# Three of eleven down-projection weight tiles of each expert multiplied in fp32 instead of as fp16 pairs

## The chip, the cores and the metric

The kernel runs on one core of one Trainium2 chip. The metric is the device time of the whole program in microseconds; lower is better. A time is the median of several runs; the profile is of one execution, whose own time stands beside its span.

## The reference, cut to what matters

A two-layer diffusion trunk over 256 latent and 256 context tokens of width 1024. The change touches the last part alone, the second layer's mixture of experts over the 256 latent tokens: eight SwiGLU experts, two for each token, each expert with a gate/up matrix (1024 x 5632) and a down matrix (2816 x 1024) in fp32.

```python
def swiglu(h, w_gu, w_dn):
    gate, up = jnp.split(h @ w_gu, 2, axis=-1)
    return (jax.nn.silu(gate) * up) @ w_dn
...
    top_logit, top_e = lax.top_k(logits, TOP_K)
    top_w = jax.nn.softmax(top_logit, axis=-1)
...
    yb = lax.map(lambda a: swiglu(a[0], w_gu[a[1]], w_dn[a[1]]), (xb, block_expert))
    yb = yb.reshape(n_rows, D) * row_w[:, None].astype(h.dtype)
    return jax.ops.segment_sum(yb, src_tok, num_segments=n).reshape(B, L, D)
```

## The kernel before, in words

**Products.** All large products of the kernel are made of three fp16 products. An fp32 operand is split into a high half (its fp16 rounding) and a low half (the rest, in fp16), and TensorE adds high x high, high x low and low x high. `split` (L264 to L268) does this for any tile: ScalarE writes the high half (`wh`, `hdh`, `yh`; line L267 in the profile), then VectorE, from the source and the high half, writes the low half (`wl`, `hdl`, `yl`; line L264 there, that of the helper `stt`).

**Weights.** The experts' weights come as tiles of 128 x 2048 fp32, 1 MB each, 33 for an expert: 22 for gate and up (one for each 128 of the 2816 hidden columns) and 11 for down. The SyncE queue loads them in order into raw buffers (twelve in the experts' part: `raw`, `raw2`, `raw3`, and the two of `hh` and `hl`); a raw buffer is free again when the split of its tile is done. A split tile is a pair of fp16 buffers, and there are `WB` = 3 such pairs, in rotation: a tile's split can begin when the pair of the tile three before it has been used by TensorE for the last time.

**One expert** (`expert`) has two stages. Gate-up: for each of 11 pairs of tiles TensorE forms gate and up for 256 hidden columns over the expert's 96 token slots (`CAP`), 48 products a tile (L320 to L322, 128x96 each). ScalarE applies SiLU (`ht`, L1220), VectorE multiplies by up (`ht`, L258), and a split writes `hdh` and `hdl`, two chunks of 128 at a time. Down: 44 chunk steps, 22 for each half of 512 output columns, four to a tile; in each the stationary operand is a chunk of the activations (128 x 96) and the moving one 128 x 512 of the weights, three products a step (L1239 to L1241). At the end of each half a split, scaled by the routing weight, writes `yh` and `yl`.

**Around it.** `gather` picks the next expert's 96 tokens by a one-hot product (`P`, `wsl`, `xg`; VectorE, TensorE and ScalarE) and is called from the middle of the down stage. `combine` adds the outputs of several experts back to the tokens: after experts 2, 5 and 6 eight jobs, one for each 128 columns, each with products (L1256) and one VectorE row (`xT`); they are handed to the next expert, which takes one for each pair of tiles. Expert 7 combines its own two halves at once. Each engine runs its instructions in an order fixed when the kernel is built. The builder works from the program's order but may move an instruction ahead where its inputs are ready, as it does with parts of `gather` and `combine`.

The part under `If(most > CAP)` handles an expert with over 96 tokens.

Of the kernel before, what the change touches and what calls it, by code (L numbers as in the profile page):

```python
# [7 lines left out]
FT = mybir.dt.float32  # L8
F16 = mybir.dt.float16
# [11 lines left out]
NF = 22  # L21
NE = 8
CAP = 96
VW = 416
WS = 2.0 ** 10
AS = 2.0 ** 3
PSC = 2.0 ** 10
US = 1.0 / (WS * AS)
EPS = 1e-6
# [70 lines left out]
def tile_width(name):  # L100
    if name in ("v0", "v1"):
        return 4 * VW
    if name == "up":
# [107 lines left out]
def moe_tiles(w_gu, w_dn, w_router):  # L211


    g = w_gu.reshape(NE, KD, 128, 2, NF, 128)
    g = g.transpose(0, 4, 2, 3, 1, 5).reshape(NE, NF, 128, 2048)
    d = w_dn.reshape(NE, 22, 128, 2, 512).transpose(0, 3, 1, 2, 4).reshape(NE, 11, 4, 128, 512)
    d = d.transpose(0, 1, 3, 2, 4).reshape(NE, 11, 128, 2048)
    return np.concatenate([g, d], axis=1).reshape(-1), np.ascontiguousarray(_blocks(w_router)).reshape(128, 64)

# [28 lines left out]
def trunk(tc, A, out):  # L248
    nc = tc.nc
    V, S, T, G = nc.vector, nc.scalar, nc.tensor, nc.gpsimd  # L250
    cnt = [0]

    def nm(p="t"):
        cnt[0] += 1
        return f"{p}{cnt[0]}"

    def mul(o, a, b):
        V.tensor_tensor(o, a, b, op=OP.mult)  # L258
# [7 lines left out]
    def split(hi, lo, src, scale):  # L266
        h = S.activation(hi, src, AF.Copy, scale=scale)  # L267
        stt(lo, src, scale, hi, OP.mult, OP.subtract)  # L268
        return h
# [31 lines left out]
    def load_raw(name, off, w=2048):  # L301
        raw = new_raw()
        nc.sync.dma_start(raw[:, :w], dram(name, off, w))
        return raw
# [4 lines left out]
    def split_w(raw, w, parts=None, step=1024):  # L309
        if parts is None:  # L310
            pool, tag, n = take("wb", wb_slots)
            parts = [pool.tile([128, 2048], F16, tag=tag + h, bufs=n, name=nm("w" + h)) for h in "hl"]
        hi, lo = parts
        for a in range(0, w, step):
            b = min(w, a + step)
            issued[0] = split(hi[:, a:b], lo[:, a:b], raw[:, a:b], WS)
        return hi, lo
# [268 lines left out]
    def mixer(pool, i, ada_q, nrm, nxt, first=None):  # L586
# [141 lines left out]
        def value(t):  # L728
            ps = pa()[:, :VW]
            ts_ = slice(t * 128, t * 128 + 128)  # L730
# [446 lines left out]
    def gather(pool, pos_e, w_e, slots):  # L1177
# [26 lines left out]
        return wsl, xg, PT  # L1204

    def expert(pool, wsl, xg, tile_of, jobs, meanwhile, halves=(lambda *y: None,) * 2):


        hdh = pool.tile([128, NF, CAP], F16, tag="hd", bufs=2, name=nm("hdh"))
        hdl = pool.tile([128, NF, CAP], F16, tag="hd", bufs=2, name=nm("hdl"))  # L1210
        for b in range(11):
            ps = pa([128, 2, 2, CAP])
            for j in range(2):
                w = tile_of(2 * b + j)
                for a in range(2):
                    for k in range(KD):
                        c = slice(1024 * a + 128 * k, 1024 * a + 128 * k + 128)
                        prod(ps[:, j, a], w[0][:, c], w[1][:, c], xg[:, k, 0], xg[:, k, 1], k == 0, k == KD - 1)
            t_ = pool.tile([128, 2, CAP], FT, tag="ht", bufs=3, name=nm("ht"))
            S.activation(t_, ps[:, :, 0], AF.Silu, scale=US)  # L1220
            mul(t_, t_, ps[:, :, 1])
            split(hdh[:, 2 * b:2 * b + 2], hdl[:, 2 * b:2 * b + 2], t_, US * AS)
            if jobs:
                jobs.pop(0)()
        while jobs:
            jobs.pop(0)()
        yh = pool.tile([CAP, D], F16, tag="yh", bufs=4, name=nm("yh"))
        yl = pool.tile([CAP, D], F16, tag="yl", bufs=4, name=nm("yl"))
        res = None
        for j in range(44):  # L1230
            n, f = divmod(j, NF)
            if j % 4 == 0:
                w = tile_of(22 + j // 4)
            if j == 12:
                res = meanwhile()
            if f == 0:
                py = pg()[:CAP]
            c = slice(512 * (j % 4), 512 * (j % 4) + 512)
            T.matmul(py, hdh[:, f], w[0][:, c], start=(f == 0), stop=False)  # L1239
            T.matmul(py, hdh[:, f], w[1][:, c], start=False, stop=False)  # L1240
            T.matmul(py, hdl[:, f], w[0][:, c], start=False, stop=(f == NF - 1))  # L1241
            if f == NF - 1:
                split(yh[:, 512 * n:512 * n + 512], yl[:, 512 * n:512 * n + 512], py, wsl[:, 0:1])
                halves[n](yh, yl)
        return yh, yl, res
# [29 lines left out]
    with tc.tile_pool(name="mo", bufs=1, reuse_waits="tile") as pool:  # L1275
        for t, raw in enumerate(ahead):
            nc.sync.dma_start(raw, dram("wm", t * 128 * 2048, 2048))
        raw_slots.extend([(px, "raw3", 1), (pool, "raw2", 5)])
        routed = route(pool)
        with tc.issue_after(n_f1.end.ins), tc.issue_after(routed.ins):  # L1280
            first = [split_w(ahead[0], 2048)]
        raw_slots.extend([(st, "hh", 1), (st, "hl", 1)])
        ys = []

        def moe_w(e, t):
            if e == 0 and t < len(ahead):
                return split_w(ahead[t], 2048) if t else first[0]
            return split_w(load_raw("wm", (33 * e + t) * 128 * 2048), 2048, step=2048)

        def slots_of(e):  # L1290
            return gather(pool, lambda t: posm[:, t, e:e + 1], lambda t: wsel[:, t, e, :], slot)

        ys, jobs = [], []
        with tc.issue_after(issued[0].ins):
            g = slots_of(0)
        for e in range(NE):
            wsl, xg, PT = g
            if e == NE - 1:
                nrm = Norm(1, 0, [(2, 4)])
                expert(pool, wsl, xg, lambda t: moe_w(e, t), jobs, lambda: None,  # L1300
                       [lambda yh, yl, n=n: [job() for job in combine([(yh, yl, PT)], nrm)[4 * n:4 * n + 4]]
                        for n in range(2)])
                break
            yh, yl, g = expert(pool, wsl, xg, lambda t: moe_w(e, t), jobs, lambda: slots_of(e + 1))
            ys.append((yh, yl, PT))
            if e in (2, 5, NE - 2):
                jobs, ys = combine(ys), []
        finish(nrm)
        del raw_slots[1:]

    most = nc.values_load(cnti[0:1, 0:1], min_val=0, max_val=NLAT)
    with tc.If(most > CAP):
        with tc.tile_pool(name="mo2", bufs=1) as pool, tc.tile_pool(name="dr", bufs=1,
                                                                    space=bass.MemoryType.DRAM) as dp:
            dpos = dp.tile([NE, 128, 2], FT, name="dpos")
            dsel = dp.tile([NE, 128, 4], F16, name="dsel")
            for e in range(NE):
                nc.sync.dma_start(dpos[e], posm[:, :, e])
                nc.sync.dma_start(dsel[e].rearrange("p (a b) -> p a b", a=2), wsel[:, :, e, :])
            wm = A["wm"].rearrange("(e t p n) -> e t p n", e=NE, t=33, p=128)  # L1320
            for first_slot in range(CAP, NLAT, CAP):
                slot2 = pool.tile([128, 128], FT, tag="slot2", name=nm("slot2"))
                V.tensor_scalar(slot2, slot, float(first_slot), None, op0=OP.add)
                with tc.For_i(0, NE, 1) as e:
                    pe = pool.tile([128, 2], FT, tag="pe", name=nm("pe"))
                    we = pool.tile([128, 2, 2], F16, tag="we", name=nm("we"))
                    nc.sync.dma_start(pe, dpos[ds(e, 1)].rearrange("o p t -> (o p) t"))
                    nc.sync.dma_start(we.rearrange("p a b -> p (a b)"), dsel[ds(e, 1)].rearrange("o p t -> (o p) t"))

                    def tile_of(t):  # L1330
                        raw = new_raw()
                        nc.sync.dma_start(raw, wm[ds(e, 1), t].rearrange("o p n -> (o p) n"))
                        return split_w(raw, 2048)

                    wsl, xg, PT = gather(pool, lambda t: pe[:, t:t + 1], lambda t: we[:, t, :], slot2)
                    yh, yl, _ = expert(pool, wsl, xg, tile_of, [], lambda: None)
                    for job in combine([(yh, yl, PT)]):
                        job()
            nrm = Norm(1, 0, [(2, 4)])
            for k in range(KD):  # L1340
                nrm.square(0, k)
            finish(nrm)
# [22 lines left out]
```

## Time and profile before

| | us |
|---|---|
| median of 3 runs | 1804.65 (1804.35 to 1805.43) |
| the profiled execution, its own time | 1798.44 |
| span of its trace | 1796.4 |
| first product of the experts | 1085.03 |
| last product of a down stage (expert 7) | 1775.38 |
| TensorE busy in the span | 1650.2 |
| VectorE busy | 1378.0 |
| ScalarE busy | 1039.5 |

Times inside the trace are microseconds from the span's start. The profile's busy share of an engine is a mean over the whole span; what an engine is worth in a stage is read from the windows and timelines of that stage. A matmul row's end is modelled: a 128x512 fp16 product shows as 0.379 us although the next can start 0.216 after it. An fp32 product shows as two records. In a timeline the bracket at the end of a row is the time for which the engine stood idle before it, and what ended that.

### The profile page before, as it was taken

The numbers are of one execution on the slowest core, as the hardware profiler recorded it, in microseconds if no ns is written. First come the engines' busy times: TensorE is split into PE (matmuls) and PEld (weight loads), VectorE is DVE, ScalarE is ACT, GpSimd is POOL, SyncE is SP. The second block draws the span as 40 slices with busy tenths as digits, with TensorE's granted clock in tenths as the row PEclk, the third lists the DMA queues.
The fourth block names the chain that finished last, engine by engine and source line by source line (L and its number), as shares of the span: only waits on it lengthen the run. The fifth ranks groups of instructions, "written<-read, shape, count | busy, mean of one in ns | idle before, by whom it ended". The sixth has DMA issues, their size and how long they took to land.

```text
span 1796.4 us, 38098 instructions
## 1 busy us (share of the span) xinstructions
PE 1650.2 (92%) x16125; PEld 1086.6 (60%) x16125; DVE 1378.0 (77%) x2201; ACT 1039.5 (58%) x1422; POOL 1.4 (0%) x7
## 2 busy tenths in 40 slices
PE   6998899999999999999778988999999999999995
PEld 2544444446644444467556877786868686868673
DVE  4678656455886545446888678999999999999996
ACT  3456646343422322233666548888878888878783
POOL 0000000000000000000000000000000000000000
PEclk9999999999999999999989988999999999999998
DMA  9254497452465545443637668999999999999980
GB/s 384 88 150 103 105 272 196 134 190 95 148 227 188 184 162 173 167 145 101 176 77 165 191 249 327 424 414 402 418 401 388 402 417 401 422 397 401 381 373 26
DMA packets 149986, 451.95 MB, mean 252 GB/s; under 512 B 92208, under 2 KB 95408, under 8 KB 103088
## 3 DMA queue, kind: packets, MB, share of 16 engines
q1 hardware_dynamic: 149376, 449.03, 68.9%
q8 instruction: 128, 2.10, 0.5%
q14 instruction: 50, 0.41, 0.1%
q10 hardware_dynamic: 432, 0.41, 0.1%
HBM read 427.38 MB, written 1.05 MB: 238 GB/s over the span
## 4 chain that ended last, share of the span: by engine, by line
PE 45%; DVE 18%; issue 12%; DMA 12%; ACT 5%; ACTq 0%; SPq 0%; DVEq 0%
DVE wl L264 10%; DMA raw<-in_wm 7%; PE pg L320 6%; PE pg L321 6%; PE pg L322 6%; PE pa L321 6%; PE pa L322 6%; PE pa L320 5%; DMA pt<-pn 3%; ACT wh L267 3%; PE pg L1240 2%; PE pg L1241 2%; PE pg L1239 2%; PE pb L935 1%; DVE ht L258 1%
## 5 line engine op out<-in xcount | busy, mean ns | idle before, releaser
L264 DVE SCALAR_TENSOR_TENSOR wl<-raw,wh 128x2048 f16<-128x2048 f32 (+1 forms) x477 | 820.9, 1735 | 54.6 <-ACT wh L267 50.6
L267 ACT ACTIVATE wh<-raw 128x2048 f16<-128x2048 f32 (+1 forms) x477 | 686.9, 1462 | 260.1 <-PE pa L321 93.1
L322 PEld LDWEIGHTS <-wl 128*128 128x128 f16 x4346 | 428.1, 99 | 176.6 <-DVE wl L264 58.0
L320 PEld LDWEIGHTS <-wh 128*128 128x128 f16 x4346 | 429.4, 99 | 133.3 <-issue 19.0
L321 PEld LDWEIGHTS <-wh 128*128 128x128 f16 x4346 | 428.6, 99 | 117.1 <-issue 9.6
L322 PE MATMUL pa<-xg,wl 128*128 128x96 f16 x2816 | 375.7, 207 | 37.0 <-DVE wl L264 36.5
L320 PE MATMUL pa<-xg,wh 128*128 128x96 f16 x2816 | 374.7, 206 | 3.7 <-ACT wh L267 3.7
L321 PE MATMUL pa<-xg,wh 128*128 128x96 f16 x2816 | 374.6, 206 | 0.0
L320 PE MATMUL pa<-hh,wh 128*128 128x512 f16 (+1 forms) x480 | 168.0, 357 | 7.5 <-ACT hh L538 7.5
L320 PE MATMUL pg<-hh,wh 128*128 128x512 f16 (+1 forms) x512 | 171.9, 336 | 2.7 <-DVE km L264 2.1
L321 PE MATMUL pg<-hl,wh 128*128 128x512 f16 (+1 forms) x512 | 171.8, 336 | 0.0
L321 PE MATMUL pa<-hl,wh 128*128 128x512 f16 (+1 forms) x480 | 170.3, 355 | 1.5 <-DVE hl L264 1.4
L322 PE MATMUL pg<-hh,wl 128*128 128x512 f16 (+1 forms) x512 | 171.2, 334 | 0.0
L322 PE MATMUL pa<-hh,wl 128*128 128x512 f16 (+1 forms) x480 | 170.0, 355 | 0.0
L1240 PE MATMUL pg<-wl,hdh 128*96 128x512 f16 x352 | 133.4, 379 | 7.9 <-DVE wl L264 7.4
L264 DVE SCALAR_TENSOR_TENSOR scr<-raw,cb 128x1024 f16<-128x1024 f32 x64 | 78.3, 1224 | 72.2 <-DMA raw<-in_ada 71.1
L1241 PE MATMUL pg<-wh,hdl 128*96 128x512 f16 x352 | 133.3, 379 | 0.0
L1239 PE MATMUL pg<-wh,hdh 128*96 128x512 f16 x352 | 132.2, 379 | 0.0
L267 ACT ACTIVATE pn<-P,sml 128x512 f16<-128x512 f32 (+1 forms) x96 | 60.7, 645 | 30.1 <-DMA pt<-pn 19.4
L264 DVE SCALAR_TENSOR_TENSOR pn<-P,sml,pn 128x512 f16<-128x512 f32 (+1 forms) x96 | 62.0, 659 | 20.9 <-ACT pn L267 19.9
L321 PE MATMUL pg<-dl,wh 128*128 128x512 f16 (+1 forms) x198 | 70.4, 355 | 0.0
L322 PE MATMUL pg<-dh,wl 128*128 128x512 f16 (+1 forms) x198 | 70.4, 355 | 0.0
(252 smaller groups left out, 1886.7 us busy)
## 6 DMA issues: line engine op xcount, KB each, us to landing
raw<-in_wm SPq DMA_DIRECT2D x264, 1024.0 KB, 8.1
raw<-in_ws SPq DMA_DIRECT2D x52, 1024.0 KB, 4.8
raw<-in_ada SPq DMA_DIRECT2D x48, 1024.0 KB, 5.2
raw<-in_ws SPq DMA_DIRECT2D x18, 768.0 KB, 5.1
raw<-in_ws SPq DMA_DIRECT2D x16, 704.0 KB, 4.1
raw<-in_ws SPq DMA_DIRECT2D x16, 640.0 KB, 4.2
raw<-in_ws SPq DMA_DIRECT2D x4, 832.0 KB, 11.6
xT<-in_xt SPq DMA_DIRECT2D x4, 512.0 KB, 6.2
```

The source lines that it names most:

```text
L258: V.tensor_tensor(o, a, b, op=OP.mult)
L264: return V.scalar_tensor_tensor(o, a, s, b, op0=op0, op1=op1, **kw)
L267: h = S.activation(hi, src, AF.Copy, scale=scale)
L320: T.matmul(ps, sh, mh, start=first, stop=False)
L321: T.matmul(ps, sh, ml, start=False, stop=False)
L322: T.matmul(ps, sl, mh, start=False, stop=last)
L935: T.matmul(py[64 * a:64 * a + 64], (vl if m == 2 else vh)[:, kt, vc:vc + 64], pts[a][:, :, (nkt if m == 1 else 0) + kt, :], start=(kt == 0 ...
L1239: T.matmul(py, hdh[:, f], w[0][:, c], start=(f == 0), stop=False)
L1240: T.matmul(py, hdh[:, f], w[1][:, c], start=False, stop=False)
L1241: T.matmul(py, hdl[:, f], w[0][:, c], start=False, stop=(f == NF - 1))
```

## The change

Of each expert's eleven down tiles, numbers 4, 5 and 10 (`DN_RAW`) are not split: `moe_w` returns the raw fp32 buffer. The six activation chunks 16 to 21 that these tiles meet (the last three pairs of gate-up) stay fp32 as well, in a new tile `hdf`, and `hdh` and `hdl` hold 16 chunks. For these twelve of the 44 chunk steps one fp32 product takes the place of three fp16 ones. The steps of the second half of the output begin with chunks 20 and 21, so that tile 5 (chunks 20 and 21 of both halves) holds only fp32 steps; the host lays the weights out in that order (`DN_STEPS`). The scale of the sums stays what it was: `hdf` keeps both scale factors of the gate-up sums, and the raw weights carry none.

```diff
+F32_FROM = 16
+DN_STEPS = [(0, f) for f in range(22)] + [(1, f) for f in (20, 21) + tuple(range(20))]
+DN_RAW = (4, 5, 10)
...
-    d = w_dn.reshape(NE, 22, 128, 2, 512).transpose(0, 3, 1, 2, 4).reshape(NE, 11, 4, 128, 512)
+    d = w_dn.reshape(NE, 22, 128, 2, 512).transpose(0, 3, 1, 2, 4)
+    d = np.stack([d[:, n, f] for n, f in DN_STEPS], axis=1).reshape(NE, 11, 4, 128, 512)
...
-        hdh = pool.tile([128, NF, CAP], F16, tag="hd", bufs=2, name=nm("hdh"))
-        hdl = pool.tile([128, NF, CAP], F16, tag="hd", bufs=2, name=nm("hdl"))
+        hdh = pool.tile([128, F32_FROM, CAP], F16, tag="hd", bufs=2, name=nm("hdh"))
+        hdl = pool.tile([128, F32_FROM, CAP], F16, tag="hd", bufs=2, name=nm("hdl"))
+        hdf = pool.tile([128, NF - F32_FROM, CAP], FT, tag="hdf", bufs=1, name=nm("hdf"))
...
-            mul(t_, t_, ps[:, :, 1])
-            split(hdh[:, 2 * b:2 * b + 2], hdl[:, 2 * b:2 * b + 2], t_, US * AS)
+            if 2 * b < F32_FROM:
+                mul(t_, t_, ps[:, :, 1])
+                split(hdh[:, 2 * b:2 * b + 2], hdl[:, 2 * b:2 * b + 2], t_, US * AS)
+            else:
+                mul(hdf[:, 2 * b - F32_FROM:2 * b - F32_FROM + 2], t_, ps[:, :, 1])
...
-        for j in range(44):
-            n, f = divmod(j, NF)
+        for j, (n, f) in enumerate(DN_STEPS):
...
-            T.matmul(py, hdh[:, f], w[0][:, c], start=(f == 0), stop=False)
-            T.matmul(py, hdh[:, f], w[1][:, c], start=False, stop=False)
-            T.matmul(py, hdl[:, f], w[0][:, c], start=False, stop=(f == NF - 1))
-            if f == NF - 1:
+            if f >= F32_FROM:
+                T.matmul(py, hdf[:, f - F32_FROM], w[:, c], start=begin, stop=end)
+            else:
+                T.matmul(py, hdh[:, f], w[0][:, c], start=begin, stop=False)
+                T.matmul(py, hdh[:, f], w[1][:, c], start=False, stop=False)
+                T.matmul(py, hdl[:, f], w[0][:, c], start=False, stop=end)
+            if end:
...
-            return split_w(load_raw("wm", (33 * e + t) * 128 * 2048), 2048, step=2048)
+            raw = load_raw("wm", (33 * e + t) * 128 * 2048)
+            return raw if t - 22 in DN_RAW else split_w(raw, 2048, step=2048)
```

## Rows read from the trace of the kernel before

**Rows 1.** The page: busy time, share and instructions of each engine

```profile
PE 1650.2 (92%) x16125; PEld 1086.6 (60%) x16125; DVE 1378.0 (77%) x2201; ACT 1039.5 (58%) x1422; POOL 1.4 (0%) x7
```

**Rows 2.** Windows: length, PE, PEld, DVE, ACT, POOL busy, clock, DMA share, GB/s

```profile
1431.94:1485.61 53.67, 48.85 (x1073) 46.11 (x1072) 53.46 (x44) 46.10 (x45) 0.00 (x0) 1.00 1.01 419
1485.61:1516.35 30.74, 29.70 (x144) 16.95 (x142) 27.65 (x17) 23.28 (x17) 0.00 (x0) 1.00 0.99 404
...
1601.39:1657.81 56.42, 52.30 (x1117) 48.99 (x1116) 56.24 (x49) 47.34 (x48) 0.00 (x0) 1.00 0.99 392
...
1688.82:1744.05 55.23, 49.21 (x1065) 46.01 (x1064) 55.02 (x46) 45.75 (x43) 0.00 (x0) 1.00 0.99 398
```

**Rows 3.** Timeline of VectorE at the end of expert 4's gate-up: start, us

```profile
1481.04 0.35 DVE L264 SCALAR_TENSOR_TENSOR hdl<-ht,hdh 128x192 f16<-128x192 f32 x1
1481.31 2.28 DVE L264 SCALAR_TENSOR_TENSOR wl<-raw,wh 128x2048 f16<-128x2048 f32 x1
1483.51 0.35 DVE L258 TENSOR_TENSOR ht<-ht,pa 128x192 f32<-128x192 f32 x1
1483.77 0.44 DVE L1182 TENSOR_SCALAR P<-cmat,posm 128x96 f16<-128x96 f32 x2
1484.13 2.28 DVE L264 SCALAR_TENSOR_TENSOR wl<-raw,wh 128x2048 f16<-128x2048 f32 x1
```

**Rows 4.** Timeline of TensorE, the last fourteen products of that gate-up

```profile
1485.02 0.21 PE L321 MATMUL pa<-xg,wh 128*128 128x96 f16 x1
...
1485.57 0.21 PE L322 MATMUL pa<-xg,wl 128*128 128x96 f16 x1
```

**Rows 5.** Timeline of ScalarE in expert 4's down stage

```profile
1501.35 0.68 ACT L267 ACTIVATE yh<-pg,wsl 96x512 f16<-96x512 f32 x1 [2.19 <-PE pg L1241]
1501.94 5.50 ACT L267 ACTIVATE wh<-raw 128x2048 f16<-128x2048 f32 x3
...
1511.37 1.91 ACT L267 ACTIVATE wh<-raw 128x2048 f16<-128x2048 f32 x1 [0.68 <-DMA raw<-in_wm]
1513.96 1.91 ACT L267 ACTIVATE wh<-raw 128x2048 f16<-128x2048 f32 x1 [0.68 <-PE pg L1241]
```

**Rows 6.** Timelines of fp32 products and stationary loads in the first layer

```profile
21.54 1.92 PE L412 MATMUL pg<-raw,c 128*32 128x512 f32 x16
...
79.33 0.59 PE L679 MATMUL pg<-rq,cmat 128*128 128x256 f32 x2
79.76 0.34 PE L320 MATMUL pa<-wh,hh 128*128 128x416 f16 x1
...
79.15 0.37 PEld L679 LDWEIGHTS pg<-rq,cmat 128*128 128x128 f32 x2
```

**Rows 7.** Timeline of TensorE, its waits in expert 4's down stage

```profile
1486.47 0.38 PE L1240 MATMUL pg<-wl,hdh 128*96 128x512 f16 x1 [0.47 <-DVE wl L264]
...
1506.21 0.38 PE L1240 MATMUL pg<-wl,hdh 128*96 128x512 f16 x1 [0.57 <-DVE wl L264]
```

**Rows 8.** Waits between 1144 and 1776: us in total, times, longest

```profile
PE pg L1240 <- DVE wl L264: 7.4, 14, 1.0
ACT wh L267 <- DMA raw<-in_wm: 4.3, 6, 1.0
```

**Rows 9.** Timeline of VectorE at the turn to expert 4

```profile
1433.70 0.74 DVE L264 SCALAR_TENSOR_TENSOR yl<-pg,wsl,yh 96x512 f16<-96x512 f32 x1
1434.66 4.49 DVE L264 SCALAR_TENSOR_TENSOR wl<-raw,wh 128x2048 f16<-128x2048 f32 x2 [0.21 <-ACT wh L267]
1439.07 0.35 DVE L258 TENSOR_TENSOR ht<-ht,pa 128x192 f32<-128x192 f32 x1
```

**Rows 10.** Timeline of VectorE at the turns to experts 6 and 7

```profile
1606.96 0.88 DVE L264 SCALAR_TENSOR_TENSOR xT<-pb,g2s,xT 128x256 f32<-128x256 f32 x2
...
1609.96 0.35 DVE L258 TENSOR_TENSOR ht<-ht,pa 128x192 f32<-128x192 f32 x1
...
1696.73 0.35 DVE L258 TENSOR_TENSOR ht<-ht,pa 128x192 f32<-128x192 f32 x1
```

More of the change, by code (lines that the diff above doesn't have):

```diff
@@ L1235, in expert @@
                 res = meanwhile()
-            if f == 0:
+            begin, end = j % NF == 0, j % NF == NF - 1
+            if begin:
                 py = pg()[:CAP]
             c = slice(512 * (j % 4), 512 * (j % 4) + 512)
-            T.matmul(py, hdh[:, f], w[0][:, c], start=(f == 0), stop=False)
-            T.matmul(py, hdh[:, f], w[1][:, c], start=False, stop=False)
-            T.matmul(py, hdl[:, f], w[0][:, c], start=False, stop=(f == NF - 1))
-            if f == NF - 1:
+            if f >= F32_FROM:
[5 more added lines that the diff above has]
+            if end:
                 split(yh[:, 512 * n:512 * n + 512], yl[:, 512 * n:512 * n + 512], py, wsl[:, 0:1])
@@ L1332, in tile_of @@
                         nc.sync.dma_start(raw, wm[ds(e, 1), t].rearrange("o p n -> (o p) n"))
-                        return split_w(raw, 2048)
+                        return raw if t - 22 in DN_RAW else split_w(raw, 2048)
                     wsl, xg, PT = gather(pool, lambda t: pe[:, t:t + 1], lambda t: we[:, t, :], slot2)
```

## The prediction

> **What bounds the kernel now.** I read the page's busy shares first. TensorE at 92% and VectorE at 77% are means over unlike stages [rows 1], so next come the windows, cut at the first product of each expert stage. Eight experts fill the last 700 us of the span. Each is a gate-up stage (22 weight tiles) and a down stage (11 tiles), and each stage has its own limit. In expert 4's gate-up VectorE is busy 53.46 of 53.67 us, and TensorE has pauses. In its down stage TensorE is busy 29.70 of 30.74 us and VectorE 27.65 [rows 2]. The clock is at its full level (1.00, the 2.4 GHz one) in all four windows.
>
> The VectorE timeline shows what a gate-up tile costs there. From the start of a `wl` to the next row is 2.20 us, and an activation row (`ht` or `hdl`) adds 0.27. Nothing stands between them [rows 3]. TensorE's rows of the same stretch lie 0.55 us apart over thirteen steps, 42 ns a product, so a tile's 48 products take 2.04 us [rows 4]: it would be ready sooner than VectorE serves it. In the down stage a tile takes TensorE 2.59 us, the distance of two `wh` rows that each wait for it [rows 5], and that is 12 products of 0.216. VectorE's 2.20 fits inside.
>
> So a microsecond of VectorE time is worth a microsecond in gate-up and little in down, and for TensorE it is the reverse. The three tiles left unsplit are all down tiles. Between the stages time is carried only by the lead in split tiles, and `WB` = 3 pairs limit that.
>
> **Part 1: dearer products.** Per expert 12 chunk steps lose 36 fp16 products: 36 x 0.216 = 7.77 us. Each gets one fp32 product. The trace has none of 96 stationary columns, but has neighbours. A 128x256 fp32 product makes two records, and from its start to that of the next fp16 product is 79.33 to 79.76, 0.43 us [rows 6]: four passes of 256 columns at the full clock. For 512 columns that makes 0.86. The 128x512 fp32 products of the early layer take 1.92 us for 16 records [rows 6]. Four run side by side in different column groups, so less the 0.17 us of drain it is 1.75 / 4 = 0.44 per record, 0.88 a product. I take 0.86: 12 x 0.86 = 10.32, so +2.55 us per expert, **+20.4** for eight. Down is TensorE's stage, so all of it is on the path. Bounds: 0.853 (columns alone) to 0.88, or +19.7 to +22.3.
>
> Each fp32 product also loads its stationary twice. The two loads of the row take 0.37 us together [rows 6] and still fit in the 0.43 between products, so I cost them at nothing. Uncovered they would add 24 x 0.19 = 4.6 us per expert. The Trainium skill (TensorE: Matmul & The Clock Gate, Weight-path perf modes) says that the fast weight load is off for fp32, which speaks against this change. The rows agree that such a load is long, 0.19 us, and with the loads left bare the sum would be some 37 us worse; with them covered, as in the row, it stays.
>
> **Part 2: three hi/lo splits of weights removed, on ScalarE and VectorE.** 3 x 2.20 us per expert, all in the down stage, where VectorE has slack. By itself this is worth nothing there. It pays through waits:
>
> *The gap in mid-down.* ScalarE's queue holds `yh` of the first half until TensorE ends that half (2.19 us idle), and three weight splits stand behind it [rows 5]. The low half of a later tile is late by that, and TensorE stops [rows 7]. The stage has 14 such waits, 7.4 us in all [rows 8]. Four are at the first product of a down stage (0.47 us each [rows 7]) and stay, since VectorE sets both of its sides. The other ten hold 5.5 us, and each hides another 0.16, a record's 0.379 less 0.216: 7.1 us. After the change the first half ends inside raw tile 5. Tiles 4 and 5 keep TensorE busy for 8 x 0.86 = 6.9 us without a split, while the pairs of tiles 6 to 8, free since tiles 1 to 3, are filled before `yh`. Tile 9 gets tile 6's pair with tiles 7 and 8 (5.2 us) for cover, against 1.91 + 2.20. So the gap goes: **-7.1** (bounds 0 and -7.1).
>
> *The lead at the turn.* Before expert 4, gate-up begins at 1431.94. VectorE ends the second new tile only at 1433.70, does `yl`, then tiles 3 and 4, done at 1439.07, 7.13 us after the turn [rows 9]. The third must wait for the last down tile's pair. After the change the last tile is raw, so the third tile takes tile 9's pair, free 4 x 0.86 = 3.4 us before the turn, and its split is done some 1 us after it. The fourth needs the first's pair: 2.04 + 0.17 of drain, `wh` 1.91, `wl` 2.20 give 6.4 us. The gain is thus 0.7, not a whole tile. VectorE idles in between. Four turns are of this kind. In two (before experts 3 and 6) two `xT` rows of the combine stand ahead, and the fourth tile is done 8.6 us after 1601.39 [rows 10]; these rows fit into the new idle time: -2.2 each. Before expert 7 it is 1696.73 - 1688.82 = 7.9 [rows 10]: -1.5. Sum 4 x 0.7 + 2 x 2.2 + 1.5 = **-8.7** (bounds 0 and -8.7). From there on VectorE sets the pace again.
>
> **Part 3: three activation splits removed.** The `mul` stays and writes `hdf` at the same size. Of the three `hdl` one stands ahead of the last gate-up tile: 0.27 x 8 = **-2.2**. The other two fall into the down stage, where VectorE's slack hides them. Without that slack they are worth 0.5 us per expert.
>
> **Part 4: raw buffers held longer, steps reordered.** A raw tile's buffer comes free when TensorE has used it rather than at its split, three tiles later at most, and the loads of the SyncE queue behind it wait. Waits for a load come to 4.3 us over all experts [rows 8], and some are put on a load only for coming last. The stage asks less of the loads than before whenever it gets no shorter (404 to 419 GB/s now [rows 2]). Cost nothing, bound +4.3. The new order of the second half keeps the count of steps.
>
> **Sum.** 20.4 - 7.1 - 8.7 - 2.2 = +2.4 us on the profiled 1798.44, so 1800.8. The median stands 6.2 above the profiled run: 1804.65 + 2.4 = **1807.0** us, +0.13%. About 0.2% (3.6 us) is what a measurement of this kernel can tell from no change.
>
> **Rivals.**
> *A, slower: ScalarE's order keeps the lead from forming.* If `yh` of the second half is queued ahead of the third new tile's `wh`, that split waits for the turn as now. The 8.7 stay out: 1815.7. It decides once `yh` stands one place too early. For it: such an order already costs 2.19 us in mid-down [rows 5]. Against: the last tile now takes 3.4 us, in which the queue has nothing else ready. Chance 0.22.
>
> *B, faster: VectorE's new idle time in the down stage takes in small work.* Of the combine, 56.42 - 53.67 = 2.75 us of gate-up in experts 3 and 6, and 55.23 - 53.67 = 1.56 in 7 [rows 2], I have counted 1.4 and 0.8. Moved whole, the rest gives 2 x 1.35 + 0.8 = 3.5; the gather's `P` rows (0.36, seven times [rows 3]) give 2.5, the four first-product waits 4 x 0.63 = 2.5. That is -8.5: 1798.5. It decides if the instruction order puts them there, which the trace of before can't show. Chance 0.20.
>
> *C, faster: VectorE's time is the bound throughout.* Then 3 x (2.20 + 0.27) = 7.4 us per expert would come through, up to the loads: 33 x 1.049 MB at 419 GB/s are 82.6 us against 53.67 + 30.74 = 84.4. -1.8 x 8: 1790. The three pairs speak against it. Chance 0.05.
>
> *D, slower: the fp32 stationary loads are not covered*, 24 x 0.19 x 8 = +36: 1843. Chance 0.05.
>
> *E, slower: the held raw buffers starve the splits*, +4.3: 1811. Chance 0.03.
>
> **How the numbers follow.** The forecast has 0.45. Its own range is 1801 to 1812 (the bounds of product price, gap and lead partly met): 0.31 within 0.2%, 0.10 slower, 0.04 faster. A gives 0.22 slower, B 0.13 faster and 0.07 same, C 0.05 faster, D and E 0.08 slower. Together: faster 0.22, same 0.38, slower 0.40. The range takes in B and A, 1797 to 1817, and leaves out C, D and the far end of A with the gap unclosed (1822.8), some 0.15.
>
> **What would show it.** Down stages longer by some 1.6 to 1.9 us where they had a gap (near 32.6 for expert 4) and gate-ups shorter by about 1.0 (near 52.7). Two fp32 records per step of 0.43 us each, with no idle time in front. No `wl` wait in mid-down. The fourth new tile done 6.4 us after the turn, with VectorE idle for some 2 us before it. VectorE's busy time falls by 8 x 7.4 = 59 us while the span stays. The forecast is wrong if gate-up keeps its 53.7 us (A), if a down stage exceeds 34 us (D), or if the `xT` and `P` rows leave gate-up (B).

## The result and the profile after

The changed kernel takes 1815.25 us (median of five runs, 1813.31 to 1820.58) against 1804.65 for the kernel before (five runs, 1802.35 to 1807.15): a ratio of 1.0064, interval 1.0046 to 1.0081. It is slower, by 10.6 us where 2.4 were forecast. The time lies within the range that was given, and nearly on the 1815.7 of rival A; the case called likeliest did not come. That it lies within half a microsecond of A is in part chance, as the terms below show.

Before the first expert product both programs issue the same instructions in the same order, yet that product comes anywhere between 1083 and 1093 us in the fourteen profiles of this study, one of each kernel, at 1083.08 in the one of before and at 1093.39 in the one of after. So everything below is taken from the expert stage alone, first gate-up product to last down product. (The 1085.03 in the table ahead of the prediction is eighteen products late; it carried no term.) That stage took 692.68 us before and takes 704.98 after, +12.3.

The window of the whole expert stage before:

```profile
1083.08:1775.76 692.68, 643.68 (x9887) 517.03 (x9884) 659.27 (x515) 558.57 (x497) 0.00 (x0) 1.00 0.95 385
```

The windows of after: gate-up and down of expert 4, and the whole expert stage.

```profile
core 0: us, PE busy (x) PEld busy (x) DVE busy (x) ACT busy (x) POOL busy (x), PEclk, DMA share, GB/s
1448.74:1502.23 53.49, 48.67 (x1073) 46.08 (x1072) 51.42 (x42) 46.02 (x43) 0.00 (x0) 1.00 0.99 409
1502.23:1535.07 32.84, 32.23 (x133) 16.44 (x130) 22.16 (x12) 17.15 (x13) 0.00 (x0) 1.00 0.96 392
1093.39:1798.37 704.98, 662.04 (x9791) 513.05 (x9788) 599.97 (x467) 508.57 (x449) 0.00 (x0) 1.00 0.93 379
```

Against [rows 2], down went from 30.74 to 32.84, and gate-up only from 53.67 to 53.49. VectorE lost 59 us of work over the stage (659.27 before), and yet the stage got longer. Over the eight experts the gate-ups fell by 2.7 us in sum (444.9 to 442.2) where 10.9 were forecast, and the downs rose by 15.0 (247.8 to 262.8) where 13.3 were.

TensorE at the end of expert 4's down stage in after: its products, then its stationary loads.

```profile
1531.42 0.38 PE L1253 MATMUL pg<-wh,hdl 128*96 128x512 f16 x1
1531.63 3.60 PE L1249 MATMUL pg<-raw,hdf 128*96 128x512 f32 x8
1535.07 0.21 PE L324 MATMUL pa<-xg,wh 128*128 128x96 f16 x1
```

```profile
1531.20 0.12 PEld L1253 LDWEIGHTS <-hdl 128*96 128x96 f16 x1
...
1532.07 0.16 PEld L1249 LDWEIGHTS pg<-raw,hdf 128*96 128x96 f32 x1 [0.27 <-issue]
1532.49 0.16 PEld L1249 LDWEIGHTS pg<-raw,hdf 128*96 128x96 f32 x1 [0.27 <-issue]
```

Eight records from 1531.63 to 1535.07 are 0.43 each, 0.86 a product, with nothing idle in front and the next stage's first product directly behind. A load takes 0.16 of every 0.43. So the first term stands as it was made: 12 x 0.86 less 7.77, +2.55 an expert. An fp32 load of 96 columns is longer than an fp16 one (0.16 against 0.12), but lies beside the products and costs nothing here. The Trainium skill (TensorE: Matmul & The Clock Gate, Weight-path perf modes) has the fast weight load on only where the weights are 128 in number and not fp32. The trace agrees as far as it goes: the fp16 loads of 128 columns in gate-up take 0.10, less than the fp16 ones of 96. By that rule no load of this down stage is fast, fp16 or fp32, so it does not speak against this change; the prediction took it to.

ScalarE in the same down stage of after, across the turn at 1535.07.

```profile
1508.78 1.91 ACT L271 ACTIVATE wh<-raw 128x2048 f16<-128x2048 f32 x1 [1.12 <-PE pg L1253]
1519.11 0.68 ACT L271 ACTIVATE yh<-pg,wsl 96x512 f16<-96x512 f32 x1 [8.42 <-PE pg L1249]
1519.70 5.63 ACT L271 ACTIVATE wh<-raw 128x2048 f16<-128x2048 f32 x3
...
1529.24 1.91 ACT L271 ACTIVATE wh<-raw 128x2048 f16<-128x2048 f32 x1 [0.79 <-PE pg L1253]
1535.27 0.68 ACT L271 ACTIVATE yh<-pg,wsl 96x512 f16<-96x512 f32 x1 [4.11 <-PE pg L1249]
1535.85 3.70 ACT L271 ACTIVATE wh<-raw 128x2048 f16<-128x2048 f32 x2
```

This is the row that decides. Only two weight tiles of the next expert are ahead of the second `yh`; the third and fourth start at 1535.85, after it, although the third tile's pair came free when tile 9 was done, at about 1531.8. For 4.11 us ScalarE holds `yh` and waits for TensorE's last product. The first `yh` now waits 8.42 where it waited 2.19 [rows 5].

VectorE at two turns of after: to expert 1, whose first product is at 1186.04, and to expert 4 (product at 1535.07).

```profile
1190.18 4.49 DVE L268 SCALAR_TENSOR_TENSOR wl<-raw,wh 128x2048 f16<-128x2048 f32 x2 [2.48 <-ACT wh L271]
...
1535.99 0.75 DVE L268 SCALAR_TENSOR_TENSOR yl<-pg,wsl,yh 96x512 f16<-96x512 f32 x1 [2.50 <-ACT yh L271]
1537.78 4.50 DVE L268 SCALAR_TENSOR_TENSOR wl<-raw,wh 128x2048 f16<-128x2048 f32 x2 [1.05 <-ACT wh L271]
1542.20 0.35 DVE L262 TENSOR_TENSOR ht<-ht,pa 128x192 f32<-128x192 f32 x1
```

At the turn to expert 4 the row behind the fourth tile starts 7.13 us after the turn, to the hundredth what it was before the change [rows 9]. At the turn to expert 1 three `wh` happen to stand ahead of `yh`; the first of the two rows is the fourth tile's and is done 1190.18 + 2.20 - 1186.04 = 6.3 us after the turn (6.4 in the forecast, whose terms add up to 6.32), and that gate-up fell by 1.26 us (54.28 to 53.02), where those of the other experts fell by 0.14 to 0.28.

Waits in the expert stage of after: us in total, times, longest.

```profile
ACT yh L271 <- PE pg L1249: 90.3, 15, 9.1
DVE yl L268 <- ACT yh L271: 62.4, 14, 7.1
ACT wh L271 <- DMA raw<-in_wm: 3.6, 1, 3.6
PE pg L1252 <- DVE wl L268: 2.9, 7, 0.6
```

The first of them before:

```profile
ACT yh L267 <- PE pg L1241: 26.6, 15, 5.6
```

TensorE's waits for `wl` in the down stages shrank from 7.4 us in 14 [rows 8] to 2.9 in 7. In their place ScalarE stands 90 us behind `yh`, and VectorE 62 us behind ScalarE: the 59 us of removed work are now idle time.

### The profile page after: what moved, and what is told of

Its sections match the earlier page's. It is cut to its first block, busy times and chain, and to the rows that moved or that the text cites. A ratio compares the mean times of both kernels' runs of the same rounds, so it can differ in the third digit from the quotient of the medians.

```text
span 1818.5 us, 37764 instructions
## 1 busy us (share of the span) xinstructions
PE 1677.2 (92%) x16029; PEld 1087.3 (60%) x16029; DVE 1318.1 (72%) x2153; ACT 989.7 (54%) x1374; POOL 1.4 (0%) x7
## 3 DMA queue, kind: packets, MB, share of 16 engines
HBM read 427.38 MB, written 1.05 MB: 236 GB/s over the span
## 4 chain that ended last, share of the span: by engine, by line
PE 53%; DVE 15%; DMA 13%; issue 7%; ACT 3%; SPq 0%; ACTq 0%; DVEq 0%
DMA raw<-in_wm 9%; DVE wl L268 8%; PE pg L324 6%; PE pg L325 6%; PE pg L326 6%; PE pa L326 6%; PE pa L325 6%; PE pa L324 6%; PE pg L1249 4%; DMA pt<-pn 4%; PE pg L1252 3%; PE pg L1253 3%; PE pg L1251 2%; ACT wh L271 2%; PE pb L939 1%
## 5 line engine op out<-in xcount | busy, mean ns | idle before, releaser
L268 DVE SCALAR_TENSOR_TENSOR wl<-raw,wh 128x2048 f16<-128x2048 f32 (+1 forms) x453 | 764.9, 1705 | 61.2 <-ACT wh L271 58.5
L271 ACT ACTIVATE wh<-raw 128x2048 f16<-128x2048 f32 (+1 forms) x453 | 641.9, 1438 | 252.6 <-PE pa L325 92.9
L1252 PE MATMUL pg<-wl,hdh 128*96 128x512 f16 x256 | 97.0, 379 | 3.4 <-DVE wl L268 2.9
L1251 PE MATMUL pg<-wh,hdh 128*96 128x512 f16 x256 | 97.0, 379 | 0.0
L1253 PE MATMUL pg<-wh,hdl 128*96 128x512 f16 x256 | 97.0, 379 | 0.0
L1249 PE MATMUL pg<-raw,hdf 128*96 128x512 f32 x192 | 85.2, 592 | 0.0
L268 DVE SCALAR_TENSOR_TENSOR pn<-P,sml,pn 128x512 f16<-128x512 f32 (+1 forms) x96 | 61.9, 658 | 20.4 <-ACT pn L271 19.3
```

The source lines that it names most:

```text
L268: return V.scalar_tensor_tensor(o, a, s, b, op0=op0, op1=op1, **kw)
L1249: T.matmul(py, hdf[:, f - F32_FROM], w[:, c], start=begin, stop=end)
L1251: T.matmul(py, hdh[:, f], w[0][:, c], start=begin, stop=False)
L1253: T.matmul(py, hdl[:, f], w[0][:, c], start=False, stop=end)
```

## The experiments

The theory after the result: the price is on TensorE's path in full, and the lead at the turn stays out because ScalarE's order puts `yh` ahead of the third new tile (rival A). Against it stand rival C (VectorE's time bounds throughout), E (held raw buffers), and, among the causes of the missing lead, the number of split pairs. The runs were taken on several chips, where the kernel before had medians of 1800.80 to 1805.21; each ratio and its interval are against the kernel before on the same chip, so versions are compared by ratio. "Stage" is the expert stage of the profiled run, then the sums of its eight gate-ups and downs, in us.

| kernel | median us | ratio (interval) | stage | gate-ups | downs |
|---|---|---|---|---|---|
| before | 1804.65 | | 692.7 | 444.9 | 247.8 |
| after | 1815.25 | 1.0064 (1.0046 to 1.0081) | 705.0 | 442.2 | 262.8 |
| order | 1812.44 | 1.0050 (1.0027 to 1.0074) | 703.2 | 440.4 | 262.8 |
| split_kept | 1817.63 | 1.0080 (1.0055 to 1.0106) | 705.0 | 442.5 | 262.5 |
| narrow | 1803.20 | 0.9999 (0.9980 to 1.0017) | 691.8 | 443.8 | 248.0 |
| tile5 | 1811.76 | 1.0049 (1.0032 to 1.0066) | 700.7 | 444.8 | 256.0 |
| raw11 | 1812.97 | 1.0057 (1.0035 to 1.0078) | 701.0 | 438.4 | 262.6 |
| pairs6 | 1811.70 | 1.0059 (1.0037 to 1.0081) | 698.1 | 435.5 | 262.6 |
| pairs6_before | 1792.83 | 0.9957 (0.9940 to 0.9974) | 684.6 | 436.0 | 248.7 |
| pairs6_order | 1808.46 | 1.0023 (1.0004 to 1.0042) | 695.8 | 432.9 | 262.9 |
| pairs6_full | 1808.84 | 1.0026 (1.0012 to 1.0040) | 697.6 | 440.7 | 256.9 |
| pairs6_full_before | 1787.70 | 0.9905 (0.9886 to 0.9925) | 677.1 | 438.7 | 238.3 |
| ahead4 | 1796.71 | 0.9970 (0.9954 to 0.9987) | 685.6 | 429.8 | 255.8 |
| ahead4_before | 1779.27 | 0.9877 (0.9853 to 0.9901) | 666.6 | 428.4 | 238.2 |

**order.** The splits of the next expert's first three tiles go ahead of the second half's `yh` in ScalarE's order, and with them the third low half ahead of `yl` in VectorE's; nothing else changes. (`issue_after` keeps the instruction inside behind another one.)

```diff
-                split(yh[:, 512 * n:512 * n + 512], yl[:, 512 * n:512 * n + 512], py, wsl[:, 0:1])
+                if n == 1 and upcoming:
+                    upcoming()
+                    with tc.issue_after(issued[0].ins):
+                        split(yh[:, 512:], yl[:, 512:], py, wsl[:, 0:1])
+                else:
+                    split(yh[:, 512 * n:512 * n + 512], yl[:, 512 * n:512 * n + 512], py, wsl[:, 0:1])
...
+        def upcoming_of(e):
+            early.update({(e, t): moe_w(e, t) for t in range(3)})
```

> The changed kernel, with the loads and splits of the next expert's first three tiles put ahead of the second half's yh in ScalarE's queue. Theory (the twelve dearer products cost TensorE some 20 us; the lead that should pay back 8.7 of them is blocked because yh stands ahead of the third new tile): six of seven turns now take the lead, the fourth new tile is done 6.4 us after the turn and not 7.1, and the time falls by 5 to 8 us against the changed kernel, to 1807 to 1810. Rival (the queue order does not matter, VectorE sets gate-up either way): no change, 1815.

VectorE's timeline of order, at the turn to expert 3 (combine; product at 1353.03) and to expert 4 (product at 1443.31).

```profile
1349.91 2.29 DVE L268 SCALAR_TENSOR_TENSOR wl<-raw,wh 128x2048 f16<-128x2048 f32 x1
1355.90 0.48 DVE L268 SCALAR_TENSOR_TENSOR xT<-pb,g2s,xT 128x256 f32<-128x256 f32 x1 [3.71 <-PE pb L1273]
1356.31 2.28 DVE L268 SCALAR_TENSOR_TENSOR wl<-raw,wh 128x2048 f16<-128x2048 f32 x1
...
1447.45 2.29 DVE L268 SCALAR_TENSOR_TENSOR wl<-raw,wh 128x2048 f16<-128x2048 f32 x1 [2.48 <-ACT wh L271]
1449.66 0.35 DVE L262 TENSOR_TENSOR ht<-ht,pa 128x192 f32<-128x192 f32 x1
```

At the plain turn the fourth tile is done 1449.66 - 1443.31 = 6.35 us after the turn, and gate-up is 52.71: 0.78 under after, where the forecast had 0.73. Rival A's mechanism is shown. But the stage gains only 1.8 us in sum, where the expectation had 5 to 8 for the whole program. At the combine turns (experts 3 and 6) gate-up got 0.55 longer: `xT` waits for a product that follows the turn, and the third `wl` stands behind it for 3.71 us, in VectorE's queue this time. The order has to be right in two queues, and of the 8.7 us this reordering gives about a fifth.

**split_kept.** The three raw tiles are split as well and the pairs not used: the work of the weight splits is back on VectorE and ScalarE, the products stay fp32.

```diff
-            return raw if t - 22 in DN_RAW else split_w(raw, 2048, step=2048)
+            w = split_w(raw, 2048, step=2048)
+            return raw if t - 22 in DN_RAW else w
```

> The changed kernel, with the three raw tiles split all the same and the split left unused, so that only the fp32 products and the order of steps differ from before. Theory (VectorE's time in the down stage is worth nothing): within 3 us of the changed kernel, 1812 to 1818. Rival (VectorE's time is the bound throughout and the change did save it): 8 x 3 x 2.20 = 53 us slower, 1868, or a large part of that.

The window of its expert stage:

```profile
1086.75:1791.79 705.04, 662.08 (x9791) 512.88 (x9788) 653.57 (x491) 553.67 (x473) 0.00 (x0) 1.00 0.93 379
```

The stage is 705.04 against 704.98, with VectorE at 653.57 busy instead of 599.97. The removed splits are worth nothing as the change stands; rival C falls.

**narrow.** Nine of an expert's twelve fp32 products run over 384 columns instead of 512, so a quarter of their columns is left out. (The expectation says ten. Of the twelve, one begins and two end a sum, and these three keep 512.) Splits, buffers and order stay those of after.

```diff
-                T.matmul(py, hdf[:, f - F32_FROM], w[:, c], start=begin, stop=end)
+                m = 512 if begin or end else 384
+                T.matmul(py[:, :m], hdf[:, f - F32_FROM], w[:, c.start:c.start + m], start=begin, stop=end)
```

> The changed kernel, with ten of the twelve fp32 products of an expert 384 columns wide in place of 512, so that each costs what three fp16 products cost (it leaves out a quarter of their columns). All buffers are held as in the changed kernel. Theory (the products' price lies whole on the path): 10 x 0.215 x 8 = 17 us faster than the changed kernel, 1798. Rival (the loss comes from raw buffers held longer or from the new queue order): it stays near 1815, at most 5 us faster.

The fp32 records of narrow by width, two to a product:

```profile
L1250 PE MATMUL pg<-raw,hdf 128*96 128x384 f32 x144 | 50.4, 486 | 0.0
L1250 PE MATMUL pg<-raw,hdf 128*96 128x512 f32 x48 | 23.2, 592 | 0.0
```

By the measured price 9 x 0.86 / 4 = 1.94 us an expert go, 15.5 in all. The downs fell by 14.8, the stage by 13.2, the time to that of before. So the price is on the path nearly whole; in mid-down a wait of 0.15 comes back in most experts, and the gate-ups are 1.6 longer in sum.

**tile5.** Only the chunks 20 and 21 stay fp32 and only tile 5 stays raw: four fp32 products an expert, no raw tile at the turn.

```diff
-F32_FROM = 16
+F32_FROM = 20
...
-DN_RAW = (4, 5, 10)
+DN_RAW = (5,)
```

> One part of the change alone: only chunks 20 and 21 stay fp32 and only tile 5 is raw, four fp32 steps of 44 for each expert. Theory: 4 x 0.21 x 8 = 7 us dearer products, less up to 5 for the gap in mid-down, no lead since the last tile is split as before: 1806 to 1812. Rival (the loss is one of the raw last tile and its held buffer): no slower than before, 1804.

The downs rose by 8.2 us over before, more than the price of four products, 4 x (0.86 - 0.65) x 8 = 6.7. So one raw tile closes no gap. Timelines of TensorE and of ScalarE of tile5 in mid-down:

```profile
1513.61 2.74 PE L1249 MATMUL pg<-raw,hdf 128*96 128x512 f32 x6
1516.19 0.38 PE L1251 MATMUL pg<-wh,hdh 128*96 128x512 f16 x1
...
1520.39 0.38 PE L1252 MATMUL pg<-wl,hdh 128*96 128x512 f16 x1 [0.79 <-DVE wl L268]
```

```profile
1515.53 0.68 ACT L271 ACTIVATE yh<-pg,wsl 96x512 f16<-96x512 f32 x1 [5.84 <-PE pg L1249]
1516.12 5.50 ACT L271 ACTIVATE wh<-raw 128x2048 f16<-128x2048 f32 x3
```

The raw tile's products delay `yh` too: it starts only at 1515.53, when 0.66 us of them are left (tile 6 begins at 1516.19), and three splits stand behind it. TensorE's wait for the first of these is 0.79, where it was 0.57 [rows 7].

**raw11.** Eleven raw buffers instead of twelve.

```diff
-        raw_slots.extend([(px, "raw3", 1), (pool, "raw2", 5)])
+        raw_slots.extend([(px, "raw3", 1), (pool, "raw2", 4)])
```

> The changed kernel with eleven raw buffers in place of twelve, so that loads have one tile less of lead. Theory (the loss is the price of the fp32 products; loads are ahead of need): no change, within 2 us of the changed kernel, and the expert stages as long as there. Rival (raw buffers held until TensorE has used them starve the splits): slower by several us more, with ScalarE waiting for loads.

The time is no longer than after's, and the steady gate-up is 53.49 again; the 4 us by which its stage is shorter lie in the gate-up of expert 0 (56.8 against 60.9); why one buffer less shortens it is open. Rival E falls for the kernel as it was changed.

**pairs6_before and pairs6.** Six split pairs instead of three, paid for with three raw buffers, on the kernel before and on the changed one. This tested what the prediction took for granted, that three pairs limit the lead.

```diff
-        raw_slots.extend([(px, "raw3", 1), (pool, "raw2", 5)])
+        raw_slots.extend([(px, "raw3", 1), (pool, "raw2", 2)])
+        wb_slots.append((pool, "w2", 3))
...
+        del wb_slots[1:]
```

> The kernel before, with six pairs of split tiles in place of three and nine raw buffers in place of twelve (the same room). Theory (each stage has its own limit because only three split tiles can be carried from one to the next): VectorE's idle time in the down stage, some 3 us for an expert, is used for later tiles; gate-up gets shorter, 15 to 23 us faster, 1782 to 1790, unless nine raw buffers are too few for the loads. Rival (the lead is not what limits): no change, 1804.

> The changed kernel with six pairs and nine raw buffers. Theory: the 7 us of VectorE time that the change saves in each down stage now reach gate-up, so this kernel gains more from the pairs than the kernel before does, 25 to 35 us, to 1780 to 1790, where loads at 33 MB for an expert begin to bind; a queue order that puts yh first still costs part of it. Rival (the dearer products are lost whatever the lead): it stays 10 us above the kernel before with six pairs.

Both gained on their own kernels (8 and 7 us of the expert stage), but only in the gate-ups of experts 0 and 1; from expert 2 on the plain ones are what they were, 53.67 and 53.49. Nor is the gain surely that of the pairs: raw11, with one raw buffer less and no extra pair, has 3.8 of pairs6's 6.7 us in these two gate-ups, and the median of pairs6 shows little of it (1.0059 against 1.0064). pairs6 ends 19 us behind pairs6_before, as its rival said. ScalarE's timeline of pairs6 at the turn to expert 4 shows why the plain gate-ups stay as they were:

```profile
1417.14 9.10 ACT L271 ACTIVATE wh<-raw 128x2048 f16<-128x2048 f32 x5
1432.60 0.68 ACT L271 ACTIVATE yh<-pg,wsl 96x512 f16<-96x512 f32 x1 [6.36 <-PE pg L1249]
1433.18 3.70 ACT L271 ACTIVATE wh<-raw 128x2048 f16<-128x2048 f32 x2
```

The order is the same as in after, with two new tiles ahead of `yh`. The five splits run through sooner, and ScalarE then waits 6.36 us with free pairs at hand. My theory that the pairs bound the lead fell: it is the queue's order that does.

**pairs6_order.** Six pairs and the order of the run order.

> The changed kernel with six pairs, nine raw buffers, and the next expert's first three tiles ahead of the second half's yh in ScalarE's queue. Theory: at most 5 us faster than with six pairs alone, since loads bind there. Rival (the queue order is the block even with six pairs): over 5 us faster than with six pairs alone.

The steady gate-up is 52.54: another 0.17 under order. With three tiles ahead of `yh` the extra pairs add next to nothing to it.

**pairs6_full and pairs6_full_before.** Six pairs; tiles 6 to 9 of the down stage are put ahead of the first `yh` and `yl`, six tiles of the next expert (five on the kernel before) ahead of the second.

```diff
+        def upcoming_of(e, n):
+            later = [(e + 1, t) for t in range(6)] if n else [(e, t) for t in range(28, 32)]
...
-                split(yh[:, 512 * n:512 * n + 512], yl[:, 512 * n:512 * n + 512], py, wsl[:, 0:1])
+                if upcoming and upcoming(n):
+                    with tc.issue_after(issued[0].ins), tc.issue_after(low[0].ins):
+                        split(yh[:, 512 * n:512 * n + 512], yl[:, 512 * n:512 * n + 512], py, wsl[:, 0:1])
```

> The changed kernel with six pairs, and on ScalarE and VectorE both halves of every output (yh, yl) queued behind the splits that could already run: tiles 6 to 9 ahead of the first half's, the next expert's first six tiles ahead of the second half's. Theory (what blocked the lead is the queue order that was fixed at build time, which six pairs alone left as it was, not the number of pairs): gate-up of experts 2 to 7 falls by 3 to 5 us each, the whole by 20 to 30 us against six pairs alone, to 1780 to 1792, where the loads bind. Rival (the fp32 products' price cannot be made good by lead): still over 1800.

> The kernel before with the same order (five of the next expert's tiles ahead of the second half's yh) and six pairs. Theory: VectorE has 3 us idle per expert to use, so it gains 8 to 16 us against six pairs alone, to 1777 to 1785; since it still makes all splits it ends near the changed kernel with that order or behind it. Rival (the raw tiles are a loss in any order): it ends 10 us or more ahead of it.

On the kernel before the down stages fell to 29.3 to 30.3 and the time by 0.95%; on the changed kernel the time is that of pairs6_order, 21 us behind, as the rival said. In both the plain gate-ups are within 0.3 us of what they were, and those with a combine grew (in pairs6_full 58.2 and 57.9 against 56.6 and 56.3 in after). ScalarE's timeline of pairs6_full at the turn to expert 4 (1432.72):

```profile
1424.31 1.91 ACT L273 ACTIVATE wh<-raw 128x2048 f16<-128x2048 f32 x1 [0.68 <-PE pg L1255]
1437.00 0.33 ACT L1228 ACTIVATE ht<-pa 128x192 f32<-128x192 f32 x1 [10.78 <-PE pa L328]
1437.23 1.90 ACT L273 ACTIVATE wh<-raw 128x2048 f16<-128x2048 f32 x1
```

The block has moved one row on: with six tiles split, the next in ScalarE's queue is the first `ht` of the new stage, which waits for TensorE's second tile, and the seventh `wh` stands behind it for 10.78 us.

**ahead4 and ahead4_before.** So the rule was applied to every row that waits for TensorE: `ht`, `hdh`, `yh` and VectorE's rows with them are queued behind the next four tiles' splits. Six pairs, on both kernels.

```diff
+        def behind(t):
+            stack = ExitStack()
+            if ahead:
+                ahead(t)
+                stack.enter_context(tc.issue_after(issued[0].ins))
+                stack.enter_context(tc.issue_after(issued_low[0].ins))
+            return stack
...
+            with behind(2 * b + 1):
+                S.activation(t_, ps[:, :, 0], AF.Silu, scale=US)
...
+                with behind(32 if n else 27):
+                    split(yh[:, 512 * n:512 * n + 512], yl[:, 512 * n:512 * n + 512], py, wsl[:, 0:1])
...
+        def ahead_of(e, t):
+            for n in range(reached[0] + 1, min(33 * e + t + 4, 33 * NE - 1) + 1):
+                early[n] = moe_w(*divmod(n, 33))
```

> The changed kernel with six pairs and four split tiles kept ahead all the time: each ht, hdh and yh (and VectorE's rows that follow them) is queued behind the splits of the four tiles after the one that TensorE multiplies. Theory (it was the queue order at every such row, ht too, that kept the saved VectorE time from gate-up): VectorE works through the turns, gate-up of experts 2 to 7 falls from 53.5 to about 47 to 49 us, the whole by 25 to 35 us against the changed kernel, to 1780 to 1790, where the loads bind. Rival (something else holds gate-up at 53 us): still over 1800.

> The kernel before with the same order and six pairs. Theory: VectorE's whole work, 81 to 82 us for an expert, becomes the bound where the period was 84.4: 1778 to 1787. The changed kernel with the same order, which saves 7 us of that work and adds 2.5 to TensorE, should then be level with it or up to 10 us faster. Rival (the dearer products still lie on the path): this one is 10 us or more faster than the changed one with the same order.

ahead4_before is the fastest of all, 1.2% under the kernel before. ahead4 is the one version of the changed kernel that beats the kernel before, by 0.3%, and 17 us behind the same order without the change. The expectation that it would be level or ahead failed. Windows of ahead4_before, then of ahead4 (gate-up and down of expert 4, expert stage):

```profile
1423.41:1474.27 50.86, 47.99 (x1074) 46.02 (x1072) 50.86 (x41) 42.02 (x41) 0.00 (x0) 1.00 1.01 424
1474.27:1504.28 30.01, 29.53 (x144) 16.94 (x142) 29.92 (x20) 26.69 (x21) 0.00 (x0) 1.00 1.01 426
1090.13:1756.71 666.58, 636.32 (x9887) 516.39 (x9884) 652.28 (x514) 547.05 (x495) 0.00 (x0) 1.00 0.97 403
```

```profile
1430.86:1480.78 49.92, 46.52 (x1073) 45.87 (x1072) 47.26 (x39) 42.48 (x41) 0.00 (x0) 1.00 0.98 408
1480.78:1512.70 31.92, 31.85 (x131) 16.25 (x129) 26.63 (x15) 20.86 (x16) 0.00 (x0) 1.00 1.01 425
1085.78:1771.43 685.65, 651.46 (x9791) 512.02 (x9788) 596.87 (x466) 501.59 (x447) 0.00 (x0) 0.99 0.95 392
```

With the better order VectorE is busy in 50.86 of 50.86 and 29.92 of 30.01 us on the kernel before: the lead is carried over, and VectorE's time bounds both stages, close to the loads' rate (424 to 426 GB/s). Here 7 us less VectorE work an expert could count at last. In ahead4 it doesn't: TensorE fills the down stage (31.85 of 31.92), the DMA engines are busy for 1.01 of it, and gate-up got only 0.9 shorter. Of the 19 us between the two stages the downs make 17.6, 2.2 an expert, near the price of 2.55; TensorE is busy in 254.4 of the 255.8 us of ahead4's eight downs, so this part is the price, and late loads have no share in it. What stays open is why the gate-ups gained nothing (429.8 against 428.4). ahead4's waits, and those of the SyncE queue:

```profile
ACT yh L274 <- PE pg L1263: 54.0, 14, 6.9
DVE xT L269 <- PE pb L1283: 37.4, 6, 11.1
ACT wh L274 <- DMA raw<-in_wm: 29.4, 31, 3.9
```

```profile
SPq L310 <- PE pg L1263: 108.9, 18, 12.4
```

In ahead4_before `yh` costs ScalarE 17.5 us in 8 waits and `xT` VectorE 10.6 in 8, and the other two are not among its main waits. The queue's wait for raw tiles that TensorE still reads was in after too (99.5 us in 21), but there ScalarE waited for a load only once (3.6 us). With the longer lead the splits catch up with the loads: rival E, which was nothing in the kernel as changed, may have a part here, beside the rows `yh` and `xT`, on which ScalarE and VectorE still wait. Which of them keeps the gate-ups from gaining was not separated.

## Why the prediction was off

**Part 1, the price, held.** +20.4 forecast; 0.86 us a product, loads covered, +20.4 by the rows of after. narrow took 14.8 of the 15.5 us of its nine narrower products out of the downs, so the price is on the path. Rival D fell.

**Part 2, the gap in mid-down, was mis-sized.** -7.1 forecast. The downs rose by 15.0, so what closed is 20.4 - 15.0 = 5.4. The waits give nearly the same: 7.4 - 2.9 = 4.5 us, and 0.16 hidden in each of the seven that went, 5.6 together. Of the ten waits that were to go two are left (0.38 and 0.52, in experts 3 and 7). The cover by tiles 4 and 5 did that, though not as reckoned: the prediction had tiles 6 to 8 split ahead of `yh`, and in after only tile 6 is; 7, 8 and 9 are the three `wh` at 1519.70, behind the 8.42 us that `yh` blocks ScalarE.

**Part 2, the lead at the turn, is the step that failed.** -8.7 forecast, at most -1.1 measured, all of it at the one turn to expert 1. (Some of that is not lead: two `P` rows and 23 products of `gather` also left that gate-up. A plain turn with the lead gains 0.78 in order.) The step said that the third tile "takes tile 9's pair, free 4 x 0.86 = 3.4 us before the turn, and its split is done some 1 us after it". The pair was free then; ScalarE was not, it held `yh` for 4.11 us. The prediction had this as rival A, at the right place and price, and gave it 0.22 because "the queue has nothing else ready" while the last tile runs. That argument looked at what is ready, but the order is fixed at build time. A second flaw was hidden behind it: the combine's `xT` rows were to fit into VectorE's new idle time, and order showed that one of them stands ahead of the third `wl` and blocks it. Even without A the term would have been nearer 3 than 8.7.

**Part 3**, `hdl`: 0.14 to 0.28 a gate-up, some -1.6 in all against -2.2. **Part 4** cost nothing, as taken (raw11).

The measured terms, 20.4 - 5.4 - 1.1 - 1.6, make the +12.3 of the expert stage, as they must, since 5.4 is a remainder. The medians differ by 10.6, and A's sum was 20.4 - 7.1 - 2.2 = 11.1: that the time came so near to A is partly luck, a gap closed by less against a lead not wholly lost and medians that differ by less than the stages. Of the observable signs the price and VectorE's 59 us came as named, and the `wl` waits of mid-down but for two; expert 4's down took 32.84 where 32.6 was named, and gate-up kept its 53.5 and so named A. Rival B has next to no support: no gate-up of a combine fell by more than 0.3 us, and before experts 3 and 6 three `xT` rows fall into the down stage where four did; only at expert 1 did `P` rows leave gate-up.

The prediction's remark that three pairs limit the lead was wrong for this order of the queues: pairs6 doubled them and the steady gate-up did not move. With the order of the run order they were worth 0.17 a gate-up; the ahead4 kernels, which keep four tiles ahead, were run with six pairs only.

## What to carry to other kernels

Work removed from a busy engine pays only if what it frees can run: before counting a lead, go through each queue that it needs in build order and look for a row that waits for a late engine (here `yh`, then `xT`, then `ht`) with ready rows behind it. When one such row is moved, find the next one before the gain is counted. Here that order (with six pairs), without the change, was worth 1.2%, twice what the change cost.

## What was not expected of the hardware

With the longer lead the loads became a limit on ScalarE in ahead4's down stage: splits that follow at once wait for tiles that arrive every 2.43 to 2.50 us (`wh` starts in expert 4's down, 1.05 MB each, 425 GB/s), where VectorE needs 2.20. And the stretch ahead of the experts varies by some 10 us between the profiled executions, as much as the whole effect of the change, so that a single span says little about it.
